# Hybrid decoder trunk on one core: the first two products of chunk 0 take the unnormed split, and chunk 0's key and query products follow them

## Chip, core and metric

One core of a Trainium2 chip runs the whole program. The metric is device time in microseconds of one execution; three runs of the kernel before gave 2816.79, 2823.07 and 2825.55 us, so its median is 2823.07 us. Lower is better.

## What is computed

One decoder layer over 2048 tokens of width 1024, in fp32. It has three sub-layers, each between an RMSNorm ahead and one behind, added to the residual. Only the first one's beginning matters here:

```python
h = rms_norm(x, norm_mix_pre)          # x * rsqrt(mean(x*x) + eps) * g, a factor per token
z = h @ w_in                           # columns: a, g (512 each), q, k, v (512 each), forget logits
u = a * jax.nn.sigmoid(g)              # then a causal depthwise convolution, a layer norm, silu
att = forgetting_attention(q, k, v, log_f)
y = concatenate([u, att]) @ w_out
x = x + rms_norm(y, norm_mix_post)     # then cross-attention into 256 memory tokens, then an MLP
```

The norm multiplies each token by one factor r and each channel by a gain g. Since r belongs to a token, (x·g·r) @ w is ((x·g) @ w)·r: a product may be made before r is known, and r put on its output.

## The kernel before, in words

**Layout.** Everything is kept channel-major: 128 channels on the partitions, tokens along the free dimension. The 2048 tokens are four chunks of 512 (`TC`); the 1024 channels are 8 tiles of 128, numbered k. A tile of 128 output channels and one chunk is one PSUM bank.

**fp32 in three products.** A number is split into a rounded high part and a remainder (`split`: ScalarE casts the high part, VectorE subtracts it). `mm3` makes, for each k, high·high, high·remainder and remainder·high, so one product group of one output tile and one chunk is 24 matmuls of 512 columns. `scaled_split` does the same with a factor per channel in it. Weights come as 512 KB raw tiles (`wr`, two buffers) on the SP queue and are split the same way (`weight`, 128x1024 at once).

**The first norm** (`normed`): ScalarE squares the eight 128x512 tiles of a chunk, VectorE adds them up (tile `nss`; the squares are `sq`), TensorE means over the channels (`token_mean`, line 182, tile `stat`), ScalarE and VectorE make the reciprocal root (`rstd`), TensorE spreads it over the partitions (`spread`, line 198). Then VectorE multiplies x by gain and factor in place, and `halves` splits the result into the tiles `h`, two channel tiles at a time.

**The product stage** (`mix_in`) handles two chunks j = 0, 1 at a time. For each t of 4 there are a gate product and a value product (`glu`: sigmoid of the first times the second, stored as `sig` to DRAM for the convolution) and a key and a query product (`qk`). Product groups of this stage rotate through two PSUM banks (`mm`).

**What sets the order.** Up to line 1021 the program is recorded with `Engine.pinned`, so ScalarE and VectorE keep program order there; the calls of `next` in `run` (lines 1005 to 1020) write that order out by hand. After that `drive` interleaves a main generator with a side generator (attention, memory, output projection) by the ratios of `SCHED`, with the convolution's taps as background, and the tile scheduler orders by priority. Pools of fixed size (`BUFS`) decide how soon a tile can be reused: four 128x512 slots `ms` (for `nss`, `sq`, `sig` here), seven `bk`, two `wr`.

In `run`, chunk 0's x is loaded first, in four pieces of 512 KB on the SP queue, then the gains, then (from `setup_late`) four zero pads of the convolution's DRAM tiles, then weights and chunk 1's x.

Of the kernel before, what the change touches and what calls it, by code (L numbers as in the profile page):

```python
# [18 lines left out]
P = 128  # L19
# [3 lines left out]
TC = 512  # L23
NCH = S // TC
# [29 lines left out]

SCHED = dict(hw=153, hb=124, hs=61, hm=42.2, r0=0.254, a0=0.346, a1=1.16, b1=0.186, m0=0.85, m1=0.986, m2=1.12,
             bm=0.102, y1=3.12, y2=2.3, y3=2.97, y4=1.95)


# [20 lines left out]
class Trunk:  # L81
# [203 lines left out]
                self.i["x"][k : k + n, :, c * TC : (c + 1) * TC].rearrange("k p t -> p k t"))  # L285
        return xs

    def normed(self, xs, g, w, stag, out=None, tags=None):

        ss = self.tile(stag, [P, w], name="nss")  # L290
        for k in range(KT):
            self.square_sum(ss, xs[k // 4][:, k % 4], k == 0, stag)
        yield 4
        r = self.token_rstd(ss, self.mean_d)
        yield 1
        r = self.spread(r)
        yield 1
        sp = self.halves(out, xs, w, tags) if tags else iter(())
        for k in range(KT):
            x = xs[k // 4][:, k % 4]  # L300
            self.v.scalar_tensor_tensor(out=x, in0=x, scalar=g[:, k : k + 1], in1=r,
                                        op0=ALU.mult, op1=ALU.mult)
            if k % 2:
                if k > 1:
                    next(sp, None)
                yield 1.2
        for _ in sp:
            pass
# [35 lines left out]
        yield 1  # L344


    def mix_in(self, h, ht, late, after):

        nc, i = self.nc, self.i
        for t in range(4):  # L350
            glu, key, query = self.glu(h, t, ht), self.qk(h, t, ht, 12), self.qk(h, t, ht, 8)
            if t == 0:
                for _ in range(4):
                    yield next(glu)
                next(late, None)
                yield next(key)
                for _ in late:
                    pass
                yield next(key)
            yield from glu  # L360
            yield from key
            yield from query
        for b in range(2):
            wv = []
            for q in range(2):
                wv.append([self.tile("mu", [P, 4, 256 + NH], F32R, name="wv") for _ in range(2)])
                self.weight(i["w_v"][b, q], [4, 256], [w[:, :, :256] for w in wv[q]])
                for l in range(0 if b else 2):
                    self.a.copy(wv[q][l][:, :, 256:], self.wf[:, l, 4 * q : 4 * q + 4])
            cols = 256 if b else 256 + NH  # L370
            wk = [(wv[k // 4][0][:, k % 4, :cols], wv[k // 4][1][:, k % 4, :cols]) for k in range(KT)]
            if b == 0:
                buf = self.tile("ms", [P, 4 * 8 * NH + P], name="gate")
                zs = [buf[:, 64 * j : 64 * j + 64].rearrange("p (t h) -> p t h", h=NH) for j in range(3)]
                zs += [buf[:, 192:256].rearrange("p (h t) -> p h t", t=8), buf[: NH * 8, 256 : 256 + P]]
            for t in range(8):
                sl = slice((t % 4) * P, (t % 4 + 1) * P)
                ps = self.ps("mm")
                self.mm3(ps[:, :cols], [(a[:, sl], bb[:, sl]) for a, bb in ht[t // 4]], wk)
                if b == 0:  # L380
                    self.add(zs[0][:, t], ps[:, 256:cols], self.bf)

                v = self.tile("ms", [P, 2, 4, DH], F32R, name="v")
                pv = ps[:, :256].rearrange("p (g e d) -> p g e d", e=2, d=DH)
                self.split(v[:, :, 0:4:3], v[:, :, 1:3], pv)
                self.store(
                    self.d_v[h][4 * b : 4 * b + 4, :, t].rearrange("h p d -> p h d"),
                    v.bitcast(F32).rearrange("p g (e l) d -> p (g e) (l d)", e=2))
                yield 2.6
                if b == 0 and t == 7:  # L390
                    self.gate(h, zs)
                if b == 1 and t == 3:
                    for _ in after:
                        pass

    def glu(self, h, t, ht):
        nc, i = self.nc, self.i
        wg = self.wtiles(i["w_in"][4 + t])
        yield 0.1
        wa = self.wtiles(i["w_in"][t])  # L400
        yield 0.1
        for j in range(2):
            ps = self.ps("mm")
            self.mm3(ps, wg, ht[j])
            sig = self.tile("ms", [P, TC], name="sig")
            self.a.activation(sig, ps, AF.Sigmoid)
            yield 5.2
            ps = self.ps("mm")
            self.mm3(ps, wa, ht[j])
            self.mul(sig, ps, sig)  # L410
            c = 2 * h + j
            self.store(self.d_u[t][:, PAD + c * TC : PAD + (c + 1) * TC], sig)
            yield 5.2
        self.conv_push(2 * h, t)
        for k in range(4 if t == 3 else 0):
            self.conv_push(2 * h + 1, k)

    def qk(self, h, t, ht, base):
        w = self.wtiles(self.i["w_in"][base + t], SIDE if t == 0 and base == 12 else MAIN)
        for j in range(2):  # L420
            ps = self.ps("mm")
            self.mm3(ps, w, ht[j])
            yield 5.1
            o = self.tile("mu", [P, 2, TC], F32R, name="qk")
            self.scaled_split(o[:, 0], o[:, 1], ps, 1.0 if base == 12 else DH ** -0.5)
            for e in range(2):
                dst = (self.d_k[t][h][e, :, :, j * TC : (j + 1) * TC] if base == 12
                       else self.d_q[t][2 * h + j][e])
                self.store(dst.rearrange("l d t -> d l t"), o[e * DH : (e + 1) * DH].bitcast(F32))
            yield 0.1  # L430
# [547 lines left out]
    def run(self):  # L978
        nc = self.nc
        self.bg = []  # L980
        self.setup()
        self.h3, self.x2, self.fin = {}, {}, {}
        xs = self.x_load(0, nc.sync.dma_start, "mk", 4)
        nc.sync.dma_start(self.g, self.i["gains"])
        h = [[] for _ in range(NCH)]
        tags = ["mk"] * 4, ["mk", "mk", "bk", "bk"]

        n0 = self.normed(xs, self.g[:, 0], TC, "ms", h[0], tags[0])
        xs = [xs] + [None] * 3

        def norm(c, *to):
            xs[c] = self.x_load(c, nc.sync.dma_start if c == 1 else self.load, "bk")
            yield 1
            yield from self.normed(xs[c], self.g[:, 0], TC, "ms" if c == 1 else "bs", *to)

        def side():
            yield from self.memory()
            yield from norm(2)
            yield from norm(3)

        def halves(c):
            yield from self.halves(h[c], xs[c], TC, tags[c % 2])

        Engine.pinned = True
        late = self.setup_late()
        next(late)
        next(n0)
        n1 = norm(1, h[1], tags[1])
        m0 = self.mix_in(0, h[:2], n1, halves(2))
        next(m0)  # L1010
        next(n0)
        next(n0)
        next(n0)
        next(m0)
        next(n1)
        self.drive(n0)
        self.drive(late)
        next(n1)
        for _ in range(4):
            next(m0)  # L1020
        Engine.pinned = False
        self.drive(m0, side(), ratio=SCHED["r0"], bg=SCHED["a0"])
        done = set()

        def tail():
            for c in range(NCH):
                yield from self.attend(c)
                while self.x2:
                    yield None
                self.conv_flush(c)  # L1030
                yield from self.mix_out(c, FIRST if c == 0 else SIDE)
                done.add(c)

        side = tail()

        def prep(c):
            while c not in done:
                next(side, None)
            yield from self.mlp_prep(c)

        m1 = self.mix_in(1, h[2:], halves(3), prep(0))
        self.drive(m1, side, ratio=SCHED["a1"], bg=SCHED["b1"], drain=False)
        self.drive(self.mlp(0, (), prep(1)), side, ratio=SCHED["m0"], bg=SCHED["bm"], drain=False)
        self.drive(self.mlp(1, self.mlp_out(0), prep(2)), side, ratio=SCHED["m1"], bg=SCHED["bm"], drain=False)
        self.drive(self.mlp(2, self.mlp_out(1), prep(3)), side, ratio=SCHED["m2"], bg=SCHED["bm"])
        self.drive(self.mlp(3, self.mlp_out(2)))
# [61 lines left out]
```

## Time and profile before

| | |
|---|---|
| median of three runs | 2823.07 us |
| the profiled execution | 2820.59 us |
| span of its trace, first to last instruction | 2818.8 us |
| TensorE busy | 2745.9 us, 97% |
| VectorE busy | 1962.6 us, 70% |
| ScalarE busy | 1372.1 us, 49% |
| DMA, mean | 141 GB/s |

The span is the time between the first and the last instruction on the core; 1.8 us of the execution lie around it. TensorE's busy time is modelled from pipelined matmuls, so a stretch counts as full when matmuls follow one another without a wait. What an engine waits for is inferred from semaphore events. Chains and tiles are named with the program's names, buffer numbers left out.

### The profile page before, as it was taken

The page shows a single profiled execution, that of the slowest core. Times are in us where ns is not written, and L with a number is a line of the kernel's source. Part 1 is how long each engine was busy: PE and PEld are TensorE (multiplying, and loading weights), DVE is VectorE, ACT ScalarE, POOL GpSimd, SP SyncE. Part 2 cuts the span into 40 slices and gives each one's busy share as a digit, 9 for nine tenths or more (in the row PEclk, how much of TensorE's full clock was granted, in tenths as well). Part 3 has the DMA queues.
Part 4 walks back from the last instruction along what each step waited for, and adds up shares of the span by engine and source line. Part 5 has one row for each costly group of instructions (what it writes and reads, how often), then busy time and mean ns, then how long its engine had stood idle before and what let it go on. Part 6 is the DMA issues. An engine that isn't in the chain of part 4 may idle for free.

```text
span 2818.8 us, 36129 instructions
## 1 busy us (share of the span) xinstructions
PE 2745.9 (97%) x13300; PEld 2255.2 (80%) x13300; DVE 1962.6 (70%) x3596; ACT 1372.1 (49%) x2171; POOL 206.1 (7%) x376
## 2 busy tenths in 40 slices
PE   7999999999999999999999999999999999999997
PEld 5889778887877888777878888778777888888886
DVE  7677876668785666787885766997875555844436
ACT  5224644346654435465654444665555445543332
POOL 0010300001110000021100001021100000000000
PEclk9999999999999999999999999999999999999999
DMA  5375645456543334455543435464524342442222
GB/s 171 117 239 161 168 135 173 141 159 198 163 145 113 135 127 146 142 171 150 156 130 123 146 114 172 128 192 140 153 97 143 131 150 77 140 136 97 92 96 83
DMA packets 141169, 398.26 MB, mean 141 GB/s; under 512 B 15264, under 2 KB 38048, under 8 KB 136128
## 3 DMA queue, kind: packets, MB, share of 16 engines
q1 hardware_dynamic: 100080, 262.40, 28.3%
q0 software_dynamic: 40912, 133.54, 16.0%
q8 instruction: 105, 1.72, 0.3%
q14 instruction: 72, 0.59, 0.1%
HBM read 330.68 MB, written 65.20 MB: 140 GB/s over the span
## 4 chain that ended last, share of the span: by engine, by line
PE 87%; DMA 5%; DVE 4%; issue 2%; ACT 2%; POOL 0%; SPq 0%; DVEq 0%; POOLq 0%; ACTq 0%
PE mm L166 20%; PE mm L165 20%; PE mm L167 20%; PE sc L167 4%; PE sc L165 4%; PE sc L166 4%; PE o L631 4%; PE pt L613 4%; PE sc L578 2%; PE sc L579 2%; DMA rb<-drs 1%; DMA ks<-dk 1%; DVE yacc L73 1%; DMA x2r<-dx 1%; PE stat L182 1%
## 5 line engine op out<-in xcount | busy, mean ns | idle before, releaser
L73 ACT CAST wh<-wr 128x1024 fp32r<-128x1024 f32 x282 | 296.3, 1051 | 664.8 <-PE mm L166 602.0
L165 PE MATMUL mm<-h,wh 128*128 128x512 f32 x1504 | 597.7, 398 | 3.4 <-ACT h L73 2.6
L167 PE MATMUL mm<-h,wl 128*128 128x512 f32 x1504 | 595.0, 396 | 0.0
L166 PE MATMUL mm<-h,wh 128*128 128x512 f32 x1504 | 592.9, 394 | 1.8 <-DVE h L73 1.8
L73 DVE TENSOR_TENSOR wl<-wr,wh 128x1024 fp32r<-128x1024 f32 x282 | 345.0, 1224 | 278.0 <-ACT wh L73 276.6
L165 PE MATMUL mm<-hid,wh 128*128 128x512 f32 x992 | 397.6, 401 | 0.9 <-DVE yacc L73 0.9
L167 PE MATMUL mm<-hid,wl 128*128 128x512 f32 x992 | 395.6, 399 | 0.0
L166 PE MATMUL mm<-hid,wh 128*128 128x512 f32 x992 | 394.2, 398 | 0.0
L73 DVE SCALAR_TENSOR_TENSOR acc<-cu,convw,acc 128x512 f32<-128x512 f32 x480 | 357.6, 747 | 5.8
L165 PEld LDWEIGHTS mm<-h,wh 128*128 128x128 f32 x1504 | 283.4, 189 | 62.1 <-ACT h L73 3.0
L166 PEld LDWEIGHTS mm<-h,wh 128*128 128x128 f32 x1504 | 283.3, 188 | 59.8 <-DVE h L73 3.3
L167 PEld LDWEIGHTS mm<-h,wl 128*128 128x128 f32 x1504 | 283.0, 188 | 59.2 <-issue 0.5
L73 DVE TENSOR_TENSOR yacc<-mm,yacc 128x512 f32<-128x512 f32 (+1 forms) x232 | 154.7, 668 | 154.5 <-PE mm L167 153.6
L73 ACT CAST pp<-pt 128x512 fp32r<-128x512 f32 (+1 forms) x288 | 158.9, 561 | 135.5 <-PE pt L613 123.2
L165 PEld LDWEIGHTS mm<-hid,wh 128*128 128x128 f32 x992 | 186.5, 188 | 43.9 <-DVE yacc L73 2.2
L167 PEld LDWEIGHTS mm<-hid,wl 128*128 128x128 f32 x992 | 186.5, 188 | 41.9 <-issue 0.2
L166 PEld LDWEIGHTS mm<-hid,wh 128*128 128x128 f32 x992 | 186.6, 188 | 40.2 <-issue 0.2
L73 DVE TENSOR_TENSOR pp<-pt,pp 128x512 fp32r<-128x512 f32 (+1 forms) x288 | 185.8, 655 | 43.3 <-ACT pp L73 41.6
L613 PE MATMUL pt<-ident,prow 128*128 128x128 f32 x1088 | 195.1, 274 | 0.7 <-ACT prow L73 0.7
L73 DVE CUSTOM_DVE_ANT_0 prow<-sc,bias 128x512 f32<-128x512 f32 (+3 forms) x288 | 166.7, 595 | 24.6 <-PE sc L579 19.0
L73 ACT ACTIVATE prow<-prow,mx 128x128 f32<-128x128 f32 (+15 forms) x128 | 154.3, 1205 | 57.5 <-DVE mx L73 56.8
L613 PEld LDWEIGHTS pt<-ident,prow 128*128 128x128 f32 x1088 | 139.7, 141 | 33.0 <-ACT prow L73 3.9
(242 smaller groups left out, 4427.6 us busy)
## 6 DMA issues: line engine op xcount, KB each, us to landing
wr<-in_w_up_dram SPq DMA_DIRECT2D x128, 512.0 KB, 3.4
wr<-in_w_down_dram SPq DMA_DIRECT2D x128, 512.0 KB, 3.5
wr<-in_w_in_dram SPq DMA_DIRECT2D x32, 512.0 KB, 4.0
q<-dq POOLq DMA_DIRECT2D x64, 256.0 KB, 6.0
wr<-in_w_out_dram SPq DMA_DIRECT2D x32, 512.0 KB, 3.5
dx<-y SPq DMA_DIRECT2D x16, 1024.0 KB, 4.4
bias<-dnc POOLq DMA_DIRECT2D x32, 512.0 KB, 5.1
x<-in_x_dram POOLq DMA_DIRECT2D x12, 1024.0 KB, 6.2
```

What stands on the lines that cost most here:

```text
L73: ins = op(*args, **kw)
L165: mm(ps, ah, bh, start=first and j == 0, stop=False)
L166: mm(ps, ah, bl, start=False, stop=False)
L167: mm(ps, al, bh, start=False, stop=last and j == n - 1)
L182: self.nc.tensor.matmul(ps[:, t : t + 1], ss[:, t * P : (t + 1) * P], mean, start=True, stop=True)
L578: nc.tensor.matmul(ps[:, :w], q[:, 0, qs], ks[:, k0 : k0 + w], start=True, stop=False)
L579: nc.tensor.matmul(ps[:, :w], q[:, 1, qs], ks[:, k0 : k0 + w], start=False, stop=True)
L613: nc.tensor.transpose(pt[:, at : at + P], prow[t][:, (k0 + k) * P : (k0 + k + 1) * P], self.ident)
L631: nc.tensor.matmul(o[:, :, q], v[:, g + k], pp[:, :, at + q.start : at + q.stop], start=g == 0 and k == 0 and (n == 0 or nk == 2), stop=g ...
```

## The change

Chunk 0's x is no longer only normed and split. First, `normed` with `raw` splits x·g, without the token factor, into the new tiles `hu` (four slots of the pool `bk`), one 128x512 tile at a time, next to the squares. The gate and the value product of t = 0 on chunk 0 take `hu`. The spread factor is copied to a new tile `rw` (pool `ms`); the gate product is multiplied by it before the sigmoid, and value times sigmoid once more. The normed split `h` of chunk 0 is still made, for everything else. Key and query products of chunk 0 follow directly (before: the key product alone, then chunk 1's gate), with their weights loaded and split earlier; the query weight's split goes into slots of the pools `bu` and `bp`. In program order the gains and the gate weight are loaded ahead of x. Two ratios of `SCHED` change: `a1` from 1.16 to 1.15 (side work in the second product stage) and `b1` from 0.186 to 0.211 (convolution taps there).

```diff
-SCHED = dict(hw=153, hb=124, hs=61, hm=42.2, r0=0.254, a0=0.346, a1=1.16, b1=0.186, m0=0.85, m1=0.986, m2=1.12,
+SCHED = dict(hw=153, hb=124, hs=61, hm=42.2, r0=0.254, a0=0.346, a1=1.15, b1=0.211, m0=0.85, m1=0.986, m2=1.12,
...
-    def normed(self, xs, g, w, stag, out=None, tags=None):
+    def normed(self, xs, g, w, stag, out=None, tags=None, raw=None):
         ss = self.tile(stag, [P, w], name="nss")
+        if raw is not None:
+            ru = self.pair8(w, "hu", ["bk"] * 4)
+            raw.extend(self.ktiles(ru))
         for k in range(KT):
-            self.square_sum(ss, xs[k // 4][:, k % 4], k == 0, stag)
+            x = xs[k // 4][:, k % 4]
+            if raw is not None:
+                self.scaled_split(ru[0][k // 4][:, k % 4], ru[1][k // 4][:, k % 4], x, g[:, k : k + 1])
+            self.square_sum(ss, x, k == 0, stag)
         yield 4
         r = self.token_rstd(ss, self.mean_d)
         yield 1
         r = self.spread(r)
+        if raw is not None:
+            self.rw = self.tile(stag, [P, w], name="rw")
+            self.a.copy(self.rw, r)
...
     def mix_in(self, h, ht, late, after, raw=None):
...
         for t in range(4):
-            glu, key, query = self.glu(h, t, ht), self.qk(h, t, ht, 12), self.qk(h, t, ht, 8)
+            glu = self.glu(h, t, ht, raw if t == 0 else None)
+            wk = wq = None
             if t == 0:
-                for _ in range(4):
+                for n in range(4):
                     yield next(glu)
+                    if n == 1:
+                        wk = self.wtiles(i["w_in"][12], SIDE)
+                        wq = self.wtiles(i["w_in"][8], dict(w=("bu", "bp")))
+            key, query = self.qk(h, t, ht, 12, wk), self.qk(h, t, ht, 8, wq)
+            if t == 0:
                 next(late, None)
                 yield next(key)
+                yield next(query)
                 for _ in late:
                     pass
                 yield next(key)
+                yield next(query)
...
     def glu(self, h, t, ht, raw=None):
...
             ps = self.ps("mm")
-            self.mm3(ps, wg, ht[j])
+            early = raw if j == 0 else None
+            self.mm3(ps, wg, early or ht[j])
             sig = self.tile("ms", [P, TC], name="sig")
+            if early:
+                self.mul(sig, ps, self.rw)
+                ps = sig
             self.a.activation(sig, ps, AF.Sigmoid)
             yield 5.2
             ps = self.ps("mm")
-            self.mm3(ps, wa, ht[j])
+            self.mm3(ps, wa, early or ht[j])
             self.mul(sig, ps, sig)
+            if early:
+                self.mul(sig, sig, self.rw)
...
         Engine.pinned = True
         late = self.setup_late()
+        n1 = norm(1, h[1], tags[1])
+        m0 = self.mix_in(0, h[:2], n1, halves(2), raw)
+        next(m0)
+        xs[0] = self.x_load(0, nc.sync.dma_start, "mk", 4)
+        n0 = self.normed(xs[0], self.g[:, 0], TC, "ms", h[0], tags[0], raw)
         next(late)
         next(n0)
-        n1 = norm(1, h[1], tags[1])
-        m0 = self.mix_in(0, h[:2], n1, halves(2))
         next(m0)
-        next(n0)
...
-        for _ in range(4):
+        for _ in range(3):
             next(m0)
```

The instructions move with it at three places. The first is ScalarE at the start, between the end of chunk 0's squares and the squares of chunk 1. Before (`sq_187` is the last square of chunk 0, `wh` are weight casts, `h_223` and `h_225` the normed split, `nss_250` the first square of chunk 1):

```order
L73 ACTIVATE sq_187<-x_150 128x512
L73 CAST wh_192<-wr_190 128x1024
L73 ACTIVATE rstd_196<-stat_197,eps 128x4
L73 CAST wh_213<-wr_211 128x1024
L73 CAST h_223<-x_149 128x1024 x2
L73 CAST h_225<-x_150 128x1024 x2
L73 CAST wf<-wfraw_165 128x64
L73 ACTIVATE nss_250<-x_217 128x512
```

Now (`hu` is the unnormed split, `xh` and `bu` are the casts of the key and the query weight):

```order
L73 ACTIVATE hu_176<-x_157,gains 128x512
L73 ACTIVATE sq_213<-x_157 128x512
L73 CAST wh_218<-wr_216 128x1024
L73 ACTIVATE rstd_222<-stat_223,eps 128x4
L73 COPY rw_235<-stat_230 128x512
L73 CAST xh_239<-wr_237 128x1024
L73 CAST bu_245<-wr_243 128x1024
L73 ACT_TABLE_LOAD
L73 ACTIVATE sig_274<-sig_274 128x512
L73 CAST h_285<-x_156 128x1024 x2
L73 CAST h_287<-x_157 128x1024 x2
```

Between the factor and the normed split stood one weight cast; now a copy, two weight casts, a table load and a sigmoid stand there. The second place is VectorE at the end of chunk 1's square sums (seven of them, the last three shown), up to its factor. Before (`mm_300` is chunk 0's value product, `xl` a weight's remainder):

```order
L73 TENSOR_TENSOR nss_250<-nss_250,sq_264 128x512
L73 TENSOR_TENSOR nss_250<-nss_250,sq_267 128x512
L73 TENSOR_TENSOR nss_250<-nss_250,sq_270 128x512
L73 TENSOR_TENSOR sig_298<-mm_300,sig_298 128x512
L73 RECIPROCAL rstd_327<-rstd_327 128x4
L73 TENSOR_TENSOR xl_338<-wr_335,xh_337 128x1024
```

Now (`mm_335` is the value product, `mm_396` the query product):

```order
L73 TENSOR_TENSOR nss_312<-nss_312,sq_326 128x512
L73 TENSOR_TENSOR nss_312<-nss_312,sq_329 128x512
L73 TENSOR_TENSOR nss_312<-nss_312,sq_332 128x512
L73 TENSOR_TENSOR sig_274<-mm_335,sig_274 128x512
L73 SCALAR_TENSOR_TENSOR qk_453<-mm_396,qk_453 128x512
L73 TENSOR_TENSOR sig_274<-sig_274,rw_235 128x512
L73 RECIPROCAL rstd_363<-rstd_363 128x4
```

The value product is now read, and `sig` and `rw` are given back, only behind the seventh sum of chunk 1. The third place is TensorE far later, in the second product stage, where the residual's factor is spread (`stat`, line 198) among the v products (`mm`, 24 matmuls each). Before, in the seventh of eight v products:

```order
L167 MATMUL mm_5364<-wv_5030,h_2699 128x264
L198 MATMUL stat_5394<-ident,rstd_5355 128x128
L165 MATMUL mm_5364<-wv_5030,h_2698 128x264
L198 MATMUL stat_5394<-ident,rstd_5355 128x128
L166 MATMUL mm_5364<-wv_5031,h_2698 128x264
```

Now, in the eighth:

```order
L165 MATMUL mm_5440<-wv_5047,h_2723 128x264
L166 MATMUL mm_5440<-wv_5048,h_2723 128x264
L198 MATMUL stat_5433<-ident,rstd_5425 128x128 x4
L167 MATMUL mm_5440<-wv_5047,h_2724 128x264
L165 MATMUL mm_5440<-wv_5047,h_2723 128x264
```

Seventeen matmuls of 264 columns that stood between this spread and the next mean (line 182, of the sum behind it) now stand ahead of the spread.

## Rows read from the trace of the kernel before

**Rows 1.** The page's head: span, then TensorE's busy time, share and instructions

```profile
span 2818.8 us, 36129 instructions
PE 2745.9 (97%) x13300; PEld 2255.2 (80%) x13300; DVE 1962.6 (70%) x3596; ACT 1372.1 (49%) x2171; POOL 206.1 (7%) x376
```

**Rows 2.** Windows: stretch, length, busy (x instructions) by engine, TensorE clock, DMA

```profile
0.00:22.00 22.00, 4.66 (x15) 3.49 (x16) 11.99 (x21) 10.41 (x15) 4.70 (x19) 1.00 0.88 294
```

**Rows 3.** Timeline of TensorE: start, duration, line, operation, [idle before <- releaser]

```profile
12.81 1.87 PE L182 MATMUL stat<-mean_d,nss 128*128 128x1 f32 x8 [12.81 <-DVE nss L73]
...
21.51 0.80 PE L166 MATMUL mm<-h,wh 128*128 128x512 f32 x1 [1.29 <-DVE h L73]
...
24.77 0.39 PE L165 MATMUL mm<-h,wh 128*128 128x512 f32 x1
25.00 0.39 PE L166 MATMUL mm<-h,wh 128*128 128x512 f32 x1
...
33.40 0.95 PE L182 MATMUL stat<-mean_d,nss 128*128 128x1 f32 x8
...
47.55 0.50 PE L166 MATMUL mm<-h,wh 128*128 128x512 f32 x1
```

**Rows 4.** Timeline of ScalarE, first 60 us

```profile
5.02 0.63 ACT L73 ACTIVATE nss<-x 128x512 f32<-128x512 f32 x1 [2.71 <-DMA x<-in_x_dram]
...
10.54 1.15 ACT L73 ACTIVATE sq<-x 128x512 f32<-128x512 f32 x2 [0.38 <-DMA x<-in_x_dram]
12.16 1.04 ACT L73 CAST wh<-wr 128x1024 fp32r<-128x1024 f32 x1 [0.46 <-DMA wr<-in_w_in_dram]
...
26.89 2.88 ACT L73 ACTIVATE sq<-x 128x512 f32<-128x512 f32 x5
29.94 0.64 ACT L73 ACTIVATE sq<-x 128x512 f32<-128x512 f32 x1 [0.16 <-DVE nss L73]
...
31.57 1.28 ACT L73 ACT_TABLE_LOAD   x1 [0.21 <-DVE nss L73]
32.87 0.60 ACT L73 ACTIVATE sig<-mm 128x512 f32<-128x512 f32 x1
...
59.90 0.60 ACT L73 ACTIVATE qk<-mm 128x512 fp32r<-128x512 f32 x1 [2.17 <-PE mm L167]
```

**Rows 5.** Timeline of VectorE, first 60 us

```profile
16.46 1.41 DVE L73 SCALAR_TENSOR_TENSOR x<-x,gains,stat 128x512 f32<-128x512 f32 x2 [1.27 <-PE stat L198]
...
25.14 2.43 DVE L73 TENSOR_TENSOR h<-x,h 128x1024 fp32r<-128x1024 f32 x2
...
27.62 5.46 DVE L73 TENSOR_TENSOR nss<-nss,sq 128x512 f32<-128x512 f32 x7
...
37.15 2.72 DVE L73 SCALAR_TENSOR_TENSOR x<-x,gains,stat 128x512 f32<-128x512 f32 x4
...
46.28 1.22 DVE L73 TENSOR_TENSOR h<-x,h 128x1024 fp32r<-128x1024 f32 x1
```

**Rows 6.** Timeline of the SP queue's issues, first 4 us

```profile
2.84 0.81 SPq L984 DMA_DIRECT2D gains<-in_gains_dram  x1
```

**Rows 7.** Timeline of VectorE where a scaled split and a square sum alternate

```profile
649.07 0.68 DVE L73 TENSOR_TENSOR ss<-ss,sq 128x512 f32<-128x512 f32 x1
649.68 0.73 DVE L73 SCALAR_TENSOR_TENSOR h<-y,gains,h 128x512 fp32r<-128x512 f32 x1
...
656.66 0.68 DVE L73 TENSOR_TENSOR ss<-ss,sq 128x512 f32<-128x512 f32 x1
```

**Rows 8.** Waits of TensorE over the whole span: total us, times, longest us

```profile
PE sc L578 <- DMA ks<-dk: 8.6, 6, 4.2
...
PE stat L182 <- DVE ss L73: 5.9, 2, 4.9
...
PE sc L578 <- DMA kv<-dk: 2.1, 2, 1.1
```

**Rows 9.** Windows, columns as in rows 2, behind a wait of 1.5 us

```profile
264.00:267.00 3.00, 3.00 (x17) 3.00 (x17) 2.51 (x3) 3.00 (x3) 0.00 (x0) 0.55 0.71 239
```

More of the change, by code (lines that the diff above doesn't have):

```diff
@@ L344, in memory, with mix_in @@
         yield 1
-    def mix_in(self, h, ht, late, after):
+    def mix_in(self, h, ht, late, after, raw=None):
         nc, i = self.nc, self.i
         for t in range(4):
-            glu, key, query = self.glu(h, t, ht), self.qk(h, t, ht, 12), self.qk(h, t, ht, 8)
+            glu = self.glu(h, t, ht, raw if t == 0 else None)
+            wk = wq = None
             if t == 0:
-                for _ in range(4):
+                for n in range(4):
                     yield next(glu)
+                    if n == 1:
[3 more added lines that the diff above has]
+            if t == 0:
                 next(late, None)
                 yield next(key)
+                yield next(query)
                 for _ in late:
@@ L394, in mix_in, with glu @@
                         pass
-    def glu(self, h, t, ht):
+    def glu(self, h, t, ht, raw=None):
         nc, i = self.nc, self.i
@@ L416, in glu, with qk @@
             self.conv_push(2 * h + 1, k)
-    def qk(self, h, t, ht, base):
-        w = self.wtiles(self.i["w_in"][base + t], SIDE if t == 0 and base == 12 else MAIN)
+    def qk(self, h, t, ht, base, w=None):
+        w = w or self.wtiles(self.i["w_in"][base + t])
         for j in range(2):
@@ L982, in run @@
         self.h3, self.x2, self.fin = {}, {}, {}
-        xs = self.x_load(0, nc.sync.dma_start, "mk", 4)
         nc.sync.dma_start(self.g, self.i["gains"])
@@ L986, in run @@
         tags = ["mk"] * 4, ["mk", "mk", "bk", "bk"]
-        n0 = self.normed(xs, self.g[:, 0], TC, "ms", h[0], tags[0])
-        xs = [xs] + [None] * 3
+        xs = [None] * NCH
+        raw = []
         def norm(c, *to):
```

## The prediction

> **What bounds the kernel.** I read the page's head first: TensorE is busy 2745.9 of 2818.8 us [rows 1], so a change pays only in the 73 us in which it is not. The windows put 17.3 of these into the first 22 us, where it is busy for 4.66 [rows 2]. The timeline of TensorE tells why [rows 3]: a mean at 12.81, and products without a wait only from about 22.1, at first 0.43 us apart (the slow clock), from 24.77 on 0.23 (24.77, 25.00). Ahead of them stand x's loads (the first quarter landed at 5.02, the last at 10.54 [rows 4]), the squares and their sum, and the norm on VectorE, which starts at 16.46 and ends its last remainder at 27.57 [rows 5]. The change aims at this idle time: its first two products need no factor. But behind them comes chunk 1's norm, and the question is how much TensorE has to do until that is ready. So I follow one milestone, six product groups done (144 matmuls): before these are gate, value and key of both chunks, now gate, value, key and query of chunk 0 and gate and value of chunk 1. Before, the sixth ended where ScalarE copies chunk 1's key product, 59.9 [rows 4].
>
> **The start, worked through.** *Loads.* Gains (0.81 us to issue [rows 6]) and a gate weight now stand ahead of x. The first quarter took 4.2 us from its issue at 0.8 to 5.02; so the weight lands near 5.4 and x's quarters some 1.9 later than before, 6.9 to 12.4 (estimate; 1 us either way). The pads' zeros now stand behind the weight's remainder on VectorE, so the SP queue waits for them until 7.7, with two weights and chunk 1's x behind; these still land by about 14 to 21, no later than ScalarE comes to them, so this costs nothing; uncovered it would cost what a weight is late.
>
> *Unnormed split and sum.* ScalarE casts the weight (1.04 [rows 4]) to 6.5, VectorE takes its remainder (1.22 [rows 5]) to 7.7. Then VectorE has eight remainders and seven sums. The nearest rows are the same pair of shapes further on: from 649.07 to 656.66 six pairs pass, 1.27 us each [rows 7]. The first remainder begins at 7.7, the second when ScalarE has its high part (8.7), seven pairs from there: the sum is ready at 17.6. Before, TensorE began its mean at 12.81 [rows 3], so the factor is 4.9 us later. TensorE meanwhile makes the gate product, paced by VectorE.
>
> *Factor to normed split.* From the mean's begin to x's norm took 3.65 us at the slow clock (12.81 to 16.46); the mean alone is 0.95 instead of 1.87 at the faster one (33.40 [rows 3]), about 1.3 less in all with the spread. I take 3.65, since nothing in these rows shows that a trickle raises the clock: 21.3. Then ScalarE copies the factor (0.60, as the sigmoid [rows 4]) and casts two weights (1.04 each), VectorE takes the second one's remainder (1.22) and puts the factor on the gate product (0.7): x's norm starts at 25.9. From there it took 11.1 us to 27.57, with one weight's remainder (1.1) inside, so 10.0; I add 0.3 because the first cast of h now waits behind a table load and the sigmoid. Normed split of chunk 0: 36.2, against 27.57. TensorE ends the value product near 27, trickles along the key product until 37.4 and then has the query product.
>
> *Chunk 1's square sums.* This is the costly step. Of the four slots `ms`, the tiles `rw`, `sig` and `nss` hold three until the value product has been multiplied by `rw`, which VectorE does behind the seventh sum. So the squares have one slot, and each waits for the sum ahead of it. Before, five squares ran through in 2.88 us, only later ones waited for a sum [rows 4], and seven sums took 5.46 us [rows 5]. Now a turn is a square (0.63), a sum (0.68) and two hand-overs, together about 0.1 (seven dependent sums in 5.46 are 0.78 each, against 0.68 of one): 1.42 us. The first sum begins at 36.4; six turns and 0.7 later the seventh ends, 45.6. Before it was 33.08.
>
> *To the end of the sixth group.* From the last square (44.9) the copy of the query product (0.60), a table load (1.28 [rows 4]) and root, reciprocal and spread (14.68 to 16.46 is 1.8 at the slow clock, I take 1.4): chunk 1's norm begins at 48.2. It began at 37.15 and its last remainder ended at 47.50 [rows 5], 10.35 us; so 58.6. Before, TensorE took its last wait for it at 47.55 [rows 3] and had 12.3 us left to the milestone; now the order leaves 16 matmuls behind the last remainder, 16 x 0.23 = 3.7. Milestone: 62.3 against 59.9, **2.4 us later**: 8.6 us of work were brought forward and 11.1 lost on the chain. Bounds: 1 us on the loads, 1.3 less with the fast clock, 1.5 more if the pairs of the first split run at 1.42 as well: 0 to 5.
>
> **What else moves.** In one go: the copy and the two extra multiplications lie beside TensorE's work once chunk 1 is there; the convolution's first load, and the memory's behind it on the POOL queue, wait for `sig`, some 13 us later, and by the order the memory is first squared near 63, which leaves it about that much; if it were late, ScalarE would wait and TensorE, with 48 matmuls at hand, not. Chunk 1's key product waits 0.2 for a bank. In the second product stage the order lets 17 matmuls pass ahead of a spread instead of behind it; at 0.118 us each (264 columns, half of 0.23) TensorE comes 2.0 us earlier to the mean that already waited 4.9 [rows 8], and VectorE's chain between has one small remainder (0.4) less: **+1.6**, 0 to 2. In the first attention chunk the order puts 16 to 32 units of 512 columns, mostly 24 or more, between the release of a key buffer and its next use, against 12 to 25 before, some 1.3 us more; the two waits of 2.1 us for `kv` [rows 8] should go: **-2.1**, -4 to 0. The faster convolution moves about a dozen taps (0.75 us, as the remainder in rows 7) forward beside TensorE's work: 0, -2 to 2. Sum: 2.4 + 0.2 + 1.6 - 2.1 = +2.1. The profiled execution took 2820.6 (its span and 1.8 us around it), so 2822.7; it lay 2.5 under the median of 2823.07, so **2825.2** in terms of the median, given as 2825.
>
> **Two rules of the Trainium skill, weighed.** Key and query product share one PSUM bank here, as the value product is still unread: the query product waits until both halves of the key's split are out, 0.6 us on ScalarE and 0.7 on VectorE behind a sum. The Trainium skill's page "Perfetto Trace Analysis", section "Matmuls", says that independent groups should rotate through different banks so that emptying one overlaps the next group's matmuls, which speaks against this order. By that rule some 1.7 us would be added, 2826.9; by the rows TensorE waits for chunk 1's sum at 45.6 anyway, and the sum stays. The table load of 1.28 us is followed by its sigmoid within 0.02 (31.57, 32.87 [rows 4]). The Trainium skill's page "ScalarE: Activation LUTs", section "What ACT_TABLE_LOAD costs", puts a drain of about 1.38 us behind the load. By that page two loads on the chain, where one was, would make it 1.4 more, 2826.6; the trace shows no such drain and decides.
>
> **Rivals.** *The early products are a plain gain.* If chunk 1's squares kept their pace and its norm were ready while TensorE still has chunk 0's 96 matmuls to make, the 8.6 us brought forward would stay, with the attention waits 10.7: 2812. Against it: the one slot for the squares; it needs chunk 1's sum by about 35. *The key loads become the wait* (slower). In the later attention chunks the order shortens two leads, from a key buffer's release to the product that needs the next load, from 41 to 21 and from 31 to 16 units (9.4 to 4.8 us, 7.1 to 3.7). By the same count a load with a lead of 16 made the wait of 4.2 [rows 8], and one of 20 elsewhere waited for nothing: it decides from about 4.5 us down. At 4.2 each this adds 8.4: 2834. For it: `ks` is already TensorE's costliest DMA wait. Against: other leads grow by 4 to 7 units. *The clock falls in the trickles.* Behind a wait of 1.5 us the granted clock was 0.55 over 3 us, mostly the lower level of 1.2 GHz [rows 9], matmuls taking twice as long. In the query product, straight after a trickle, this would cost some 1.6, and again at chunk 1: 2828. *It does little*: the first product waits for late gains or a late weight, 3 us more: 2828 as well.
>
> **How the numbers follow.** A measurement of this kernel can tell some 0.3%, 8.5 us, from no change: under 2814.6 is faster, over 2831.5 slower. Forecast 0.55, clock or late start 0.15, a milder sum in which the start breaks even and the attention waits shrink (2819) 0.06: all within 0.3%, together 0.76. Plain gain 0.10. Key loads 0.14, slower. The range of 2815 to 2835 takes in all but the plain gain, the key loads' far end and what may happen in the reordered middle.
>
> **What would show it.** First product on `hu` at 7 to 8 us; chunk 0's sum at 17 to 18.5; chunk 1's squares six times behind a sum, the seventh sum near 46; chunk 1's key product copied near 68 (62.3 and 24 matmuls). The mean near 650 us waits 6 to 7 us. No `kv` wait near 320 to 350. Wrong would be: chunk 1's sum ready by 40, or `ks` waits far above 8.6 us in all.

## The result, and the profile after

Four runs of the changed kernel gave a median of 2846.62 us, against 2821.92 of the kernel before run beside it: ratio 1.0087, 95% interval 1.0069 to 1.0105. That is 24.6 us slower, where 2825 was forecast, within 0.3%. The page's head of the changed kernel:

```profile
span 2845.4 us, 36125 instructions
...
PE 2760.5 (97%) x13300; PEld 2263.4 (80%) x13300; DVE 1971.2 (69%) x3606; ACT 1378.4 (48%) x2180; POOL 209.5 (7%) x376
```

Against [rows 1] the span is 26.6 us longer and TensorE busy 14.6 us longer with the same 13300 matmuls. So TensorE waits 12 us more, and it is also slower while busy: the granted clock must have fallen somewhere.

To see where the time went, I compared the times at which both traces had done the same number of matmul columns; this is what "lost by" and "loses" mean from here on. The distance of the two traces grows by 6.5 us in the first 100 us of the kernel before, by 1.5 to 295, **by 16.7 from 295 to 415**, by -0.1 to 640, 4.2 to 700, -2.9 to 1420, -4.7 to 2100, 5.3 to 2200 and -0.6 to 2800; the sum is 25.9 of the 26.6. Windows of TensorE in the kernel before (stretch, length, busy, clock, DMA share, GB/s):

```profile
0.00:100.00 100.00, 80.64 (x360) 1.00 0.47 150
...
295.00:415.00 120.00, 113.07 (x540) 0.99 0.59 162
```

and in the changed kernel:

```profile
0.00:100.00 100.00, 80.35 (x320) 0.93 0.45 142
...
295.00:415.00 120.00, 103.93 (x474) 0.90 0.61 159
303.00:439.70 136.70, 120.63 (x542) 0.91 0.54 146
...
640.00:700.00 60.00, 51.46 (x355) 0.91 0.55 173
...
2100.00:2200.00 100.00, 96.31 (x444) 0.97 0.38 118
```

In the first 100 us TensorE is as busy as before, but makes 320 matmuls instead of 360, at a granted clock of 0.93. (The column reads 1.00 also ahead of 24.4 us, where the kernel before has matmuls 0.43 us apart; so it leaves out the slow matmuls at the very start.) From 295 to 415, in the first attention chunk, it is busy for 9 us less and its clock is 0.90 instead of 0.99. The work that the kernel before does there takes the changed one from 303.0 to 439.7: 9.1 us more of idle time, and 7.6 more of busy time for as many matmuls, at a clock of 0.91. What it waits for there (290 to 420 us: us in total, times, longest):

```profile
PE sc L604 <- DMA q<-dq: 6.9, 3, 2.8
PE sc L604 <- DMA kv<-dk: 2.9, 1, 2.9
PE pt L639 <- ACT prow L73: 2.2, 1, 2.2
PE mm L165 <- ACT sig L73: 1.6, 1, 1.6
```

The kernel before has no wait for `q` there; its longest is 1.4. One of the three, with what follows it, on TensorE's timeline:

```profile
309.62 0.47 PE L166 MATMUL mm<-h,xh 128*128 128x512 f32 x1
312.86 0.30 PE L604 MATMUL sc<-kv,q 128*128 128x128 f32 x1 [2.77 <-DMA q<-dq]
...
313.65 0.63 PE L165 MATMUL mm<-h,xh 128*128 128x512 f32 x1
314.07 0.63 PE L166 MATMUL mm<-h,xh 128*128 128x512 f32 x1
```

Behind the wait matmuls of 512 columns begin 0.42 us apart, where 0.23 is the distance at the full clock. So the waits cost nearly twice what they last: 16.7 us for 9.1 of idle time.

**Why `q` is late.** The tiles `q` of an attention chunk rotate through the pool `bu`, which has two slots. `mix_in` runs twice, for chunks 0 and 1 and for chunks 2 and 3, and the change's line `wq = self.wtiles(..., dict(w=("bu", "bp")))` stands in both. In the second call the query weight takes one of the two slots, in the trace from its cast at 279.3 to the last product that reads it at 385.0. From the second head on all heads' `q` share the other: the next load starts only when the last score product of the head ahead has read it. That product, and the two loads of the next head's `q` (timelines of TensorE and of the POOL queue):

```profile
301.93 0.39 PE L605 MATMUL sc<-kv,q 128*128 128x512 f32 x1
...
302.61 0.62 POOL L123 DMA_DIRECT2D q<-dq  x1 [6.96 <-PE sc L605]
306.29 0.61 POOL L123 DMA_DIRECT2D q<-dq  x1
```

The products at 312.86 are the ones that waited for them. In the kernel before, the load that the score products at 310.08 read was issued at 293.92, a whole head earlier. Between the release of a `q` slot and its next use TensorE did 47 to 59 units there (a unit is one 512-column matmul), now 6 to 32. A rotation of two became one without a line of the attention code being touched. The Trainium skill's page "Trainium Kernel Development and Optimization", section "Best Practices", asks for double buffers so that loads overlap work; the trace agrees with the page, with 6.9 us of waits for `q` where there were none.

The weight's remainder also takes one of the two slots `bp`, through which attention's split probabilities (`pp`) rotate. The waits on TensorE do not point there (for `pp` 0.3 us in this stretch, 1.5 in the kernel before); the first two runs below move both slots at once, the last pair `bu` alone.

The start, on VectorE's timeline of the changed kernel:

```profile
26.02 2.71 DVE L73 SCALAR_TENSOR_TENSOR x<-x,gains,stat 128x512 f32<-128x512 f32 x4
...
43.53 0.69 DVE L73 TENSOR_TENSOR nss<-nss,sq 128x512 f32<-128x512 f32 x1 [0.70 <-ACT sq L73]
44.93 0.69 DVE L73 TENSOR_TENSOR nss<-nss,sq 128x512 f32<-128x512 f32 x1 [0.70 <-ACT sq L73]
...
48.87 2.72 DVE L73 SCALAR_TENSOR_TENSOR x<-x,gains,stat 128x512 f32<-128x512 f32 x4 [1.21 <-PE stat L198]
...
58.01 1.22 DVE L73 TENSOR_TENSOR h<-x,h 128x1024 fp32r<-128x1024 f32 x1
```

This chain came nearly as worked out: chunk 0's norm at 26.02 (25.9 forecast), a turn of chunk 1's squares 1.40 us (1.42), the seventh sum out at 45.6 (45.6), chunk 1's norm at 48.87 (48.2), its last remainder at 59.2 (58.6). What differs is TensorE in the gate product of chunk 1:

```profile
51.41 1.22 PE L165 MATMUL mm<-h,wh 128*128 128x512 f32 x2 [2.57 <-ACT h L73]
52.78 0.79 PE L166 MATMUL mm<-h,wh 128*128 128x512 f32 x1 [0.15 <-DVE h L73]
53.37 0.63 PE L167 MATMUL mm<-h,wl 128*128 128x512 f32 x1
...
57.62 0.40 PE L165 MATMUL mm<-h,wh 128*128 128x512 f32 x1
```

From 52.78 it waits for nothing, but its matmuls are 0.43 us apart until 57.6: after 45.2 it had little to do for 6 us, and the clock was at the lower level of 1.2 GHz. The sixth group's last matmul ended at 65.7 instead of 59.9.

### The profile page after: what moved, and what is told of

The parts are those of the page before. It is cut to its first block, busy times and chain, and to the rows that moved or that the text cites. A ratio compares the mean times of both kernels' runs of the same rounds, so it can differ in the third digit from the quotient of the medians.

```text
span 2845.4 us, 36125 instructions
## 1 busy us (share of the span) xinstructions
PE 2760.5 (97%) x13300; PEld 2263.4 (80%) x13300; DVE 1971.2 (69%) x3606; ACT 1378.4 (48%) x2180; POOL 209.5 (7%) x376
## 4 chain that ended last, share of the span: by engine, by line
PE 86%; DMA 5%; DVE 5%; issue 2%; ACT 2%; POOL 0%; SPq 0%; DVEq 0%; POOLq 0%; ACTq 0%
PE mm L165 19%; PE mm L166 19%; PE mm L167 19%; PE sc L167 4%; PE sc L165 4%; PE sc L166 4%; PE o L657 4%; PE pt L639 4%; PE sc L604 2%; PE sc L605 2%; DMA q<-dq 1%; DMA ks<-dk 1%; DMA x<-in_x_dram 1%; DVE yacc L73 1%; PE stat L182 1%
## 5 line engine op out<-in xcount | busy, mean ns | idle before, releaser
L165 PE MATMUL mm<-h,wh 128*128 128x512 f32 x1456 | 580.0, 399 | 9.0 <-ACT relu L73 3.6
L166 PE MATMUL mm<-h,wh 128*128 128x512 f32 x1456 | 577.4, 397 | 0.6 <-DVE h L73 0.6
L167 PE MATMUL mm<-h,wl 128*128 128x512 f32 x1456 | 577.2, 396 | 0.4 <-DVE wl L73 0.4
L165 PEld LDWEIGHTS mm<-h,wh 128*128 128x128 f32 x1456 | 275.2, 189 | 67.3 <-ACT relu L73 4.0
L167 PEld LDWEIGHTS mm<-h,wl 128*128 128x128 f32 x1456 | 275.0, 189 | 58.1 <-DVE wl L73 0.8
L166 PEld LDWEIGHTS mm<-h,wh 128*128 128x128 f32 x1456 | 275.3, 189 | 56.7 <-DVE h L73 1.6
```

What stands on the lines that cost most here:

```text
L165: mm(ps, ah, bh, start=first and j == 0, stop=False)
L166: mm(ps, ah, bl, start=False, stop=False)
L167: mm(ps, al, bh, start=False, stop=last and j == n - 1)
```

## The experiments

All ratios are to the kernel before, run beside each, with their 95% interval; us are the ratio's part above 1 times 2822.

**The slot, given back and taken away.** e1: the changed kernel, the second stage's query weight in another pool.

```diff
-  wq = self.wtiles(i["w_in"][8], dict(w=("bu", "bp")))
+  wq = self.wtiles(i["w_in"][8], dict(w=("bu", "bp") if h == 0 else ("mu", "mu")))
```

> The changed kernel, except that in the second product stage the early query weight takes slots of the pool mu instead of bu and bp. In the changed kernel that weight holds one of the two bu slots from its load until the first attention chunk is nearly done, so the tiles q of that attention chunk share one slot. Theory (lost slot): the three q waits of 6.9 us between 310 and 362 us and the slow clock behind them go, 12 to 18 us less than the changed kernel, 2829 to 2835. Rival (ratios a1 and b1 moved attention products): stays at 2846. Rival (moving the key and query products of the second stage forward is what hurts): stays at 2846 too, since that order is kept.

1.0040 (1.0025 to 1.0055), 11.3 us over the kernel before: 13.3 of the 24.6 are gone. Waits of e1 from 290 to 420 us, then its window:

```profile
PE o L657 <- ACT h L73: 3.3, 1, 3.3
PE sc L604 <- DVE mx L73: 3.1, 2, 1.6
...
PE sc L604 <- DMA kv<-dk: 1.5, 3, 0.6
```

```profile
295.00:415.00 120.00, 106.75 (x507) 0.94 0.57 155
```

No `q` wait is left. The stretch still loses 9.2 us, now to several smaller waits, and between 700 and 1420 6.6 us come back (2.9 in the changed kernel).

e2: the kernel before, with the second stage's query weight loaded early into the two slots, and nothing else.

```diff
-                for _ in range(4):
+                for n in range(4):
                     yield next(glu)
+                    if n == 1 and h == 1:
+                        wq = self.wtiles(i["w_in"][8], dict(w=("bu", "bp")))
+                        query = self.qk(h, t, ht, 8, wq)
```

> The kernel before, except that the query weight of the second stage's first group is loaded and split early into slots of bu and bp, as in the changed kernel; order of products, start and ratios stay. Theory (lost slot): q waits of TensorE appear between 300 and 370 us, 10 to 18 us slower than the kernel before, 2832 to 2840. Rivals (ratios, start, order of products): within 3 us of the kernel before, 2822.

1.0045 (1.0030 to 1.0061), 12.7 us slower, and the waits are there:

```profile
PE sc L581 <- issue: 4.9, 1, 4.9
PE sc L581 <- DMA q<-dq: 4.2, 2, 3.1
PE pt L616 <- ACT prow L73: 2.5, 1, 2.5
```

The wait of 4.9 us for which no release is shown ("issue") ended at 355.73, 0.1 behind the landing of a `q` load at 355.63, so it belongs to `q` as well. Some 13 us from both sides, each to within 4 to 6 us: the lost slots are the larger half of the result.

**The start alone.** e3: second stage as in the kernel before (key product alone moved ahead, query weight in its old place; but the key weight is still loaded two products earlier), ratios a1 and b1 as before. e4: the same with `rw` in the pool `vk`.

```diff
-  self.rw = self.tile(stag, [P, w], name="rw")
+  self.rw = self.tile("vk", [P, w], name="rw")
```

> The changed start alone: second product stage in the order and with the weight slots of the kernel before, ratios a1 and b1 of the kernel before. Theory: only the late start is left, about +6 at 60 us (slow clock in chunk 1's gate product, 12 matmuls at 0.43 instead of 0.23, and chunk 1's sum at 45.6), so 2826 to 2830. Rival (the ratios cost it): 2820 to 2823. Rival (the start also disturbs what follows): over 2832.

> As the run with the changed start alone, but the factor tile rw lies in the pool vk, so that chunk 1's squares have two slots of ms and not one. Theory (one slot paces chunk 1's squares): a turn falls from 1.39 us to 0.75 to 0.8, chunk 1's seventh sum ends near 42 instead of 45.6, the sixth product group 3 to 4 us earlier, 3 to 4 us less than the start alone. Rival (ScalarE and VectorE are paced by the normed split and the copy of the key product anyway): within 1 us of the start alone.

e3: 1.0041 (1.0027 to 1.0056), 11.6 us, twice what was expected: 6.1 lost by 100 us, 6.6 more from 295 to 415. e4: 1.0041 (1.0028 to 1.0054), the same. Its squares run as expected:

```profile
36.04 3.07 DVE L73 TENSOR_TENSOR nss<-nss,sq 128x512 f32<-128x512 f32 x4
...
39.63 2.27 DVE L73 TENSOR_TENSOR nss<-nss,sq 128x512 f32<-128x512 f32 x3
...
45.72 2.72 DVE L73 SCALAR_TENSOR_TENSOR x<-x,gains,stat 128x512 f32<-128x512 f32 x4 [2.14 <-PE stat L198]
```

0.76 us a turn, the seventh sum at 41.9, the norm 3.1 us earlier, the loss at 100 us 3.3 instead of 6.1. That one slot paced the squares is shown; the 2.8 us do not show at the end, where an interval of some 4 us either way could hide them.

**The clock at the start.** e11: e3 with 20 transposes of 128 columns, read by nobody, behind the spread of chunk 1's factor.

> The run with the changed start alone, and 20 transposes of 128 columns whose result nobody reads, right behind the spread of chunk 1's factor, so that TensorE is not idle for the 2.6 us until chunk 1's first split is out. Theory (TensorE's clock falls to the lower level in that wait, and the gate product's first 12 matmuls then take 0.43 instead of 0.23 us): the granted clock stays near 1 from 51 to 57 us and the sixth product group comes 2 to 3 us earlier, 2 to 3 us less than the start alone. Rival (the clock does not follow the idle time, or these products wait for VectorE's remainders anyway): same time within 1 us at 100 us.

Windows of e3, then of e11:

```profile
51.00:54.00 3.00, 2.37 (x5) 0.50 0.58 155
54.00:57.00 3.00, 3.00 (x10) 0.57 0.88 288
```

```profile
51.00:54.00 3.00, 2.36 (x10) 1.00 0.45 112
54.00:57.00 3.00, 3.00 (x15) 1.00 0.81 273
```

The clock stays up. With the transposes not counted as work, the loss at 100 us is 3.8 instead of 6.1, and the sixth group ends at 63.0 instead of 65.3: 2.3 us of the loss were the clock, as expected. At the end none of it shows: 1.0052 (1.0035 to 1.0069). The seven runs of e11 spread from 2829.7 to 2844.3; the one in the trace, the second fastest, ended 3.0 us ahead of e3's.

**The two ratios.** e5: both on the kernel before; e9 and e10: b1 and a1 alone.

> The kernel before with the two new ratios alone (a1 1.15, b1 0.211). Theory (the loss is the lost slot, the late start and the moved first attention chunk): the ratios leave the first attention chunk's key leads as they were and only shorten two leads of the later chunks from 41 to 21 and 31 to 16 units, so within 4 us of the kernel before, 2818 to 2826. Rival (key loads of the later chunks become the wait): over 2828.

1.0057 (1.0044 to 1.0071), 16.1 us: far outside what was expected. Two waits on TensorE's timeline stand out:

```profile
370.35 2.05 PE L463 MATMUL stat<-tot,ones 128*128 128x512 f32 x2 [4.89 <-DVE tot L73]
...
388.08 1.11 PE L198 MATMUL stat<-ident,rstd 128*128 128x128 f32 x4 [3.49 <-DVE rstd L73]
```

Both belong to the convolution's layer norm, which the order now puts ahead of what VectorE has done.

> The kernel before with the new share of convolution taps alone (b1 0.211). The run with both ratios waited 4.9 us for the convolution's layer norm (tot from VectorE) near 366 us and 3.5 us for a reciprocal root near 385, which the kernel before does not. Theory (faster taps bring the convolution's sums ahead of what VectorE can do): most of the 15 us of both ratios, 2832 to 2838, with those two waits. Rival (a1 does it): 2820 to 2825 without them.

> The kernel before with the new share of side work alone (a1 1.15). Theory (b1 is what costs): within 4 us of the kernel before, 2818 to 2826. Rival (a1: the two leads of the later chunks that fall from 41 to 21 and from 31 to 16 units): 2828 or more, with ks waits near 1370 and 1930 us.

b1 alone 1.0006 (0.9996 to 1.0016), a1 alone 1.0001 (0.9993 to 1.0010), neither with those waits. Each alone is free, both together cost 16 us: the price belongs to the order that comes out, not to a number. What the pair costs with the changed kernel's products is not shown: e1 has it, e3 not, and both lose some 11.5, but they differ in the moved query product too. From 2100 to 2200 e1 loses 4.3 us behind a wait of 3.5 for `relu`, e3 0.8 without it; the changed kernel loses 5.3 there (wait 3.6) and the trace of e10, the slowest of its eleven runs, 5.6 (wait 3.4). The shortened `ks` leads of e10 cost nothing that shows.

**The moved side work.** The changed start leaves one product fewer to the interleaved part, so the side work lags. e8 and e12: the kernel before with r0 0.246 and 0.262 instead of 0.254. e6 and e13: the changed start alone with 0.266 and 0.275; e14: e13 with the 20 transposes.

> The kernel before with r0 0.246 instead of 0.254 and nothing else: the side work of the first product stage comes a little later, and by the order the key loads of the first attention chunk get the leads that the changed start gives them (15 and 7 units where the kernel before has 25 and 16). Theory (the changed start moves the interleaving, and that costs 6 to 8 us between 300 and 420 us): 5 to 8 us slower than the kernel before, 2827 to 2831, with kv waits there. Rival (it is the late start itself that makes the attention chunk wait): 2820 to 2824.

1.0023 (1.0012 to 1.0034), 6.5 us slower; its waits from 290 to 420 us:

```profile
PE mm L165 <- ACT sig L73: 2.6, 1, 2.6
PE sc L578 <- DMA kv<-dk: 2.1, 3, 1.0
PE pt L613 <- ACT prow L73: 2.1, 1, 2.1
```

The waits for `sig` and `prow` are also the changed kernel's; the `kv` wait is no longer than in [rows 8].

> The kernel before with r0 0.262 instead of 0.254, the same 3% as in the run with 0.246, but the other way; the key leads of the first attention chunk stay as they were but for one unit. Theory A (the kernel before lies at a tuned place, and any shift of the side work costs): 3 to 8 us slower, 2825 to 2831, lost between 300 and 420 us. Theory B (only the shortened key leads cost, or only side work that comes later): 2820 to 2824.

1.0002 (0.9993 to 1.0011): side work that comes one such step earlier is free, one step later costs.

> As the run with the changed start alone, but r0, the share of side work in the first product stage, is 0.266 instead of 0.254. The changed start has one product fewer in the interleaved part, so that the side work ahead of the first attention chunk lags; there, counted in units of one 512-column matmul along the order, the leads of key loads fell to 14 and 7 (before 25 and 16); with 0.266 they are 19 or more again but for one of 13. Theory (moved order shortens the leads of the first attention chunk): its 7.6 us between 300 and 400 us go, the late start of 6 us stays, 2826 to 2829. Rival (the attention chunk is slower because of the late start itself, or by chance): 2833 to 2836, as before.

> The changed start alone with r0 0.275, so that the side work of the first product stage comes earlier than in the kernel before and not later; the key leads of the first attention chunk are 19 units or more but for one of 13. Theory A (what the start alone loses beyond its late start comes from side work that comes later, as in the kernel before with 0.246; earlier side work costs nothing, as with 0.262): 2826 to 2829, the late start's 6 us alone. Theory B (with the changed start the attention chunk is arranged worse whatever the share): 2831 to 2836.

> As the last, with the 20 transposes behind the spread of chunk 1's factor that kept TensorE's clock up. Theory (what the start loses at 100 us is lost at the end as well): 3 to 4 us less than the last, 2823 to 2826. Rival (later waits take up such a difference): within 1.5 us of the last.

1.0037 (1.0024 to 1.0050), 1.0031 (1.0018 to 1.0044) and 1.0035 (1.0023 to 1.0048). Earlier side work gives 1 to 3 us of the 11.6 back, which is within the noise, and not 6, although in e13's trace the stretch from 295 to 415 is 2.4 us shorter than in the kernel before: the loss then sits elsewhere, 5.2 us between 1420 and 2100. And the 2.0 us that e14 is ahead of e13 at 100 us again do not show at the end. In e14 the 20 transposes took 3.81 us instead of 2.35, and the clock was 0.68 from 51 to 54 us: they did not keep it up as in e11. My account by key leads falls: they were restored, and the time was not.

**Another order of the start.** e7: chunk 1's square sums and factor ahead of chunk 0's norm, `rw` in `vk` and read by the norm, key product read out ahead of chunk 1's norm, r0 0.266, and the second stage's key weight back in its old place. In `run`, `n1` steps through its sums and root around the third step of `m0`:

```diff
+        next(n1)
+        next(n1)
         next(m0)
         next(n1)
+        next(m0)
         self.drive(n0)
         self.drive(late)
-        next(n1)
```

> As the last, but chunk 1's square sums and factor come ahead of chunk 0's norm, rw lies in the pool vk and chunk 0's norm reads it there, and the key product is read out ahead of chunk 1's norm. Theory (the start is lost because chunk 1's norm waits for its sums behind chunk 0's split): chunk 0's norm starts near 29 instead of 26, chunk 1's near 43 instead of 48.9, its last remainder near 53, sixth product group near 56 to 57 instead of 65.7 (59.7 in the kernel before): 8 to 9 us less than the last, 3 less than the kernel before, 2817 to 2820. Rival (VectorE is full there, so that the sums only move the wait to chunk 0): 2824 or more.

1.0028 (1.0016 to 1.0039). VectorE's timeline:

```profile
22.52 5.47 DVE L73 TENSOR_TENSOR nss<-nss,sq 128x512 f32<-128x512 f32 x7 [2.47 <-ACT sq L73]
...
30.84 2.73 DVE L73 SCALAR_TENSOR_TENSOR x<-x,gains,rw 128x512 f32<-128x512 f32 x4
...
44.16 2.71 DVE L73 SCALAR_TENSOR_TENSOR x<-x,gains,stat 128x512 f32<-128x512 f32 x4
```

VectorE has hardly a gap from 22.5 to 54.5. Chunk 1's norm starts 4.7 us earlier than in the changed kernel, but chunk 0's 4.8 later, and the order leaves 30 matmuls behind the last remainder; the sixth group is done at 61.5, still behind 59.9. Eight scaled remainders of `hu` are 6 us of VectorE that the kernel before does not have; VectorE has no gap there to take them in, and that is what the early products cost.

**A third slot.** e15 and e16: `bu` 3 and `mu` 4 instead of 2 and 5, in the kernel before and in the changed one.

> The kernel before with three slots bu instead of two, paid for with one of the five slots mu (memory is full). If the number of q slots still binds in the kernel before, its first attention chunk gains and it beats both kernels: 2815 to 2820. If two slots are enough there, as the absence of q waits in its trace says: 2820 to 2825; if the fifth slot mu was needed in the MLP, slower, over 2830.

> The changed kernel with three slots bu, and four mu. Theory (lost slot): as with the weight in mu, 10 to 14 us less than the changed kernel, 2832 to 2836, plus whatever the fifth slot mu was worth (the kernel before with the same exchange tells it). Rival: stays at 2846.

1.0059 (1.0043 to 1.0075) and 1.0055 (1.0039 to 1.0072). In the kernel before the exchange costs 16.6 us and a third `bu` gains nothing that shows; the changed one gains 9 us by the same exchange. Here `bu` alone was given back and `bp` not: e16 has no `q` wait, and from 295 to 415 it loses 2.9 us against e15, where the changed kernel lost 16.7 against the kernel before. So the slot of `q` is what cost. With the exchange the changed and the unchanged kernel are level (medians 2837.05 and 2838.05), although the changed one is 3.6 us behind at 100 us. No version beat the kernel before.

## Why the prediction was wrong

- **The failed step** is in the part on what else moves: "the two waits of 2.1 us for `kv` should go: -2.1, -4 to 0". I had counted the leads of key buffers and of nothing else. The stretch lost 16.7 us, and the `kv` waits did not go either: one of 2.9 us stood for two of 2.1 in all. The section on the change said that the query weight takes slots of `bu` and `bp`; I did not ask who else lives in `bu`, nor that `mix_in` runs a second time, beside the attention. The price is some 13 us, by e1 and by e2. Neither of the two signs by which I would have known the prediction wrong came (chunk 1's sum ready by 40, `ks` waits far above 8.6 us): both watched the places that I had already thought of.
- **The start**: the chain on ScalarE and VectorE was right to 0.7 us at each point but one, the milestone was not (65.7, forecast 62.3). The one point is chunk 0's sum, out at 18.6 and not 17.6; it did no harm by luck, as the mean and its spread took 2.5 us at the full clock and not the 3.65 that I had put in for the slow one. The step that failed is "16 matmuls behind the last remainder, 16 x 0.23": at 59.2 TensorE had some 28 left, since the slow clock and not the remainders held it up. The rival on the clock named the effect; it took 1.6 us in the query product and as much at chunk 1. The query product ran at full speed (39.85, 40.08), and chunk 1 paid 2.3 (e11).
- **That a milestone's loss is the end's loss** was assumed without a word. Three pairs speak against it: e4, e11 and e14 are 2.0 to 2.8 us better at 100 us than e3, e3 and e13, and no better at the end. One such pair is within the noise; that none of the three shows a gain is the argument.
- **Sign and rivals.** The rival on the slower side, key loads, had the right side and nearly the right kind (a buffer's lead in attention), but named `ks` of the later chunks. These waits fell from 8.6 us [rows 8] to 5.6, and e10 has the same shortened leads at no cost. "0, -2 to 2" for the moved taps was much too narrow for a change of two ratios (e5).
- **The mean near 650 us** waits 6.5 us, as forecast (6 to 7). The stretch loses 4.2 and not 1.6, with two smaller waits and a clock of 0.91 against 0.94.
- **The shared bank and the table load.** The query product stood 1.41 us for the key's bank, until 39.51. As worked out, it cost nothing: chunk 1's sum was waited for behind it, for 0.52. The rule on banks of the Trainium skill's page "Perfetto Trace Analysis", section "Matmuls", is borne out as a wait. The table load was followed by its sigmoid within 0.02 us again (26.18, 1.28 long, then 27.48). So the drain that the Trainium skill's page "ScalarE: Activation LUTs", section "What ACT_TABLE_LOAD costs", states does not show here either.

**Open.** Of the 11.6 us of the start alone, 6.1 are seen at the start and 6.6 in the first attention chunk. Later side work alone can cost 6.5 (e8), but undoing it gave back 1 to 3 (e6, e13), and taking microseconds off the start gave none that shows (e4, e11, e14). Which of the many small order differences carries the rest is not settled. A single trace cannot settle it: twelve runs of e13 lie between 2823.0 and 2841.3 us.

## What to carry to other kernels

When a tile is put into a pool that has a free slot where you look, list every other user of that pool and every call of the function: here a slot held for 106 us beside a two-slot rotation cost 13 us, more than the 8.6 us of work that were to be brought forward. Work brought forward is paid for on the engine that prepares it; ask whether that engine had room. In a kernel whose order is tuned by ratios, allow for a loss of up to some 0.6% by any shift of the interleaving (here 0.0, 0.2 and 0.6%) until a run with that shift alone says otherwise.

## What the runs showed that was not expected

- Two ratios that are free one by one (1.0006 and 1.0001) cost 0.57% together.
- The waits in the first attention chunk cost TensorE nearly twice: 9.1 us of idle time, then 7.6 of matmuls at the lower clock level. Twenty transposes of 128 columns in a wait of 2.6 us kept the clock at 1.00 in e11, where it had been 0.50; in e14 it was 0.68 with the same transposes.
- Stretches give back what earlier ones lost: e1 is 15.8 us behind at 415 and gains 4.7 between 1200 and 1420, where the kernel before waits 4.2 for `ks` [rows 8].
